# Other start addresses for the operands of the down projection in a one-core decoder layer

## The chip, the cores and the metric

The kernel runs on one core of a Trainium2 chip. The metric is the device time of one execution in microseconds; where several runs are given, the median counts. Before the change, three runs took 328.39, 328.74 and 328.99 us.

## The reference

One hybrid decoder layer on 256 tokens of width 1024, all in float32. The part that matters here is its last third, the gated feed-forward network with a causal convolution of three taps:

```python
h2 = rmsnorm(x, norm_ffn_g)
up = causal_depthwise_conv(h2 @ w_up, conv_w, conv_b)
gate, val = jnp.split(up, 2, axis=-1)
return x + (jax.nn.silu(gate) * val) @ w_down
```

`w_up` is 1024 x 5632 and `w_down` 2816 x 1024. Ahead of it stand the projections of queries, keys, values, pooling input and gates, an attention of 8 heads, a causal pooling mixer, two branch projections and the output projection.

## The kernel before

**Every product is made of three.** Each float32 operand is split into a rounded high part and the rest, a low part, both in the one-pass format `float32r`. ACT writes the high part (`high`, L91), DVE the low part (`low`, L95 and L97), and TensorE adds three matmuls into one accumulator: high x high, and the two mixed products. So weights arrive by DMA in a `raw` tile and are held as a `hi_` and a `lo_` tile. From the pooling input on, the weights are the stationary operand (128 x 128) and the activations, transposed, the moving operand (128 partitions x 256 tokens). For queries, keys and values it is the other way round: there the weights move, 512 columns or, in the first two of eight steps of the queries, 256 columns at a time.

**Weights come in chunks of 1 MB** in one fixed order. In the feed-forward part the order alternates up chunks (22, one per block of 128 gate and 128 value features) and down chunks (11, each for two blocks of 128 of the 2816 features). Four buffers each hold raw, high and low parts and rotate. The function `ahead` lets ACT and DVE split chunks ahead of their use; `chunk` hands the next one to the matmuls.

**The feed-forward loop** runs i from 0 to 21. Each turn makes two up tiles, gate and value, of 24 matmuls each (3 x 8 slices of the depth), whose moving operands are `hhi` and `hlo`. DVE, ACT and POOL apply the norm's factor, the taps, the silu and the product of gate and value. `value_done` then has ACT write the high part of the result, `ah`, and `finish`, one turn later, has POOL write the low part, `al`: 256 columns of 4 bytes, 1,024 bytes in each partition. `LAG` is 3: in turn i, the matmuls of `down(i - 3)` follow the up tiles. One such block has 24 matmuls: for each of eight output slices, `hi` x `ah`, `hi` x `al` and `lo` x `ah` (L866 to L868). Block i uses down chunk i // 2, its first half for even i. Blocks 0 to 17 are followed by up tiles; 18 to 21 come at the end, the last two interleaved slice by slice. `ah` and `al` have `LAG + 2` = 5 buffers each, which rotate.

**The order of the work** on each engine is the order in which the program is written; an engine's instructions are chained so. Nothing is reordered by a planner.

**Places in memory.** Tiles lie at fixed bytes in each partition, given by the allocator in the order of the pools. The kernel shifts some operands inside their tiles by whole words of 4 bytes: `MOVING` (48 words) for the weights of queries, keys and values, `FAR` (96 words) for all other low parts. The starts before, in bytes modulo 128, as they stand in the built program:

| operand | start modulo 128 |
|---|---|
| `xhi`, `xlo`, `hhi`, `hlo`, `mh`, `ml`, `ah`, `al` and the other activations | 96 |
| high and low parts of the weights of queries, keys, values | 96 |
| high and low parts of all other weights | 32 |
| `ones_r` (two matmuls into `ps_n`, for the second norm) | 0 |

Steps inside a weight tile from one 128-column slice to the next are 512 bytes, so all slices of a tile start alike modulo 128.

Of the kernel before, what the change touches and what calls it, by code (L numbers as in the profile page):

```python
# [8 lines left out]
F32R = mybir.dt.float32r  # L9
# [4 lines left out]
P = 128  # L14
S = 256
# [31 lines left out]
LAG = 3  # L47
# [17 lines left out]
FAR = 96  # L65
MOVING = 48
XCUTS = (1, 2, 3, 4, 5, 6, 8)


@with_exitstack  # L70
def hybrid_layer_kernel(ctx: ExitStack, tc: tile.TileContext, xq_d, xtok_d, par_d, wkv_d, wpg_d,
# [12 lines left out]
    tmp = mixer.enter_context(tc.tile_pool(name="tmp", bufs=2))  # L84
# [5 lines left out]
    def high(hi, src, scale=1.0):  # L90
        nc.scalar.activation(hi, src, AF.Copy, scale=scale)  # L91
# [16 lines left out]
    order = [("q", None)] * 2 + [("k", wkv_d[c]) for c in range(2)]  # L108
# [28 lines left out]
    def raw(c, sl):  # L137

        if order[c][0] != "q":
            return raws[c][:, sl]  # L140
        at = sl.start % 512
        return xq[:, 4 * c + sl.start // 512, S + at:S + at + sl.stop - sl.start]
# [7 lines left out]
    for c in range(len(order) - 1):  # L150
        if order[c][0] == "dn" and order[c + 1][0] == "up":
            i = next(n for n, p in enumerate(pieces) if p[0] == c)
# [7 lines left out]
    def oldest():  # L160

        return next((c for c in range(len(order)) if c not in spent), len(order))

    def next_high():
        if at[0] < len(pieces):
            c, sl, first, _ = pieces[at[0]]
            if c - oldest() >= WBUFS:
                return
            at[0] += 1
            if first:  # L170
                moving = order[c][0] in "qkv"
                place = MOVING if moving else 0
                his[c] = whi_p.tile([P, CH + P], F32R, tag="whi", name=f"hi_{order[c][0]}{c}")[:, place:]
                place = MOVING if moving else FAR
                los[c] = wlo_p.tile([P, CH + P], F32R, tag="wlo", name=f"lo_{order[c][0]}{c}")[:, place:]
            high(his[c][:, sl], raw(c, sl))

# [21 lines left out]
    def ahead(upto=0):  # L199

        next_high()
        next_low()
        if at[1] - sum(p[0] < used[0] for p in pieces) < upto:
            next_high()
            next_low()
# [23 lines left out]
    cut = 0  # L229
    for k in XCUTS:  # L230
        end = KD + k * (S + AW)
# [32 lines left out]
    for k in range(KD):  # L264
        if k < HALVED:
            nc.vector.tensor_scalar(xhi[:, k, :], xT[:, k, :], gmix[:, k:k + 1], None, op0=ALU.mult)
        else:
            high(xhi[:, k, :], xT[:, k, :], gmix[:, k:k + 1])
        low(xlo[:, k, :], xhi[:, k, :], xT[:, k, :], gmix[:, k:k + 1])
        for _ in range(2 if k < HALVED else 1):  # L270
            next_high()
        for _ in range(2 if k < HALVED else 1):
            next_low(eager=True)
# [403 lines left out]
    for n in range(2 * KD):  # L677
# [13 lines left out]
        b, c = n // 2, n % 2  # L691
# [9 lines left out]
        f = 2 * GATES[b] + c  # L701
# [41 lines left out]
    tmp = ctx.enter_context(tc.tile_pool(name="ffn", bufs=2))  # L743
# [71 lines left out]
    acch, accl = {}, {}  # L815
# [12 lines left out]
    def taps(u, f, c):  # L828
        cw = [par[:, C_CW + j * 2 * KF + f:C_CW + j * 2 * KF + f + 1] for j in range(3)]
        nc.vector.scalar_tensor_tensor(c[:, 1:S], u[:, 0:S - 1], cw[1], c[:, 1:S], ALU.mult, ALU.add)  # L830
        nc.vector.scalar_tensor_tensor(c[:, 2:S], u[:, 0:S - 2], cw[0], c[:, 2:S], ALU.mult, ALU.add)  # L831
# [14 lines left out]
    def value_done(i, g, uc):  # L846
        taps(uc[0], KF + i, uc[1])
        nc.gpsimd.tensor_tensor(uc[1], g[1], uc[1], ALU.mult)  # L848
        acch[i] = tmp.tile([P, S], F32R, tag="ah", bufs=LAG + 2, name=f"ah{i}")
        accl[i] = tmp.tile([P, S], F32R, tag="al", bufs=LAG + 2, name=f"al{i}")  # L850
        high(acch[i], uc[1])
        return uc[1]

# [44 lines left out]
    ahead()  # L898
    gate_done(0, ug)
    done = value_done(0, ug, uv)  # L900
    for i in range(1, KF):
        if i > 1:
            w = chunk("up")
            ps = [up_tile(w, 0, i)]
        ug = normed(ps[0], i, f"g{i}")
        ahead()
        finish(i - 1, done)
        ps.append(up_tile(w, 1, i))
        uv = normed(ps[1], KF + i, f"v{i}")
        gate_done(i, ug)  # L910
        ahead()
        if i >= LAG:
            if i == LAG:
                pairs.close()
                down_p = ctx.enter_context(tc.tile_pool(name="down", bufs=1, space=bass.MemoryType.PSUM))
                acc += [down_p.tile([P, 512], F32, name=f"ps_d{n}") for n in range(4)]
            down(i - LAG, range(KD))
            ahead(FFN_AHEAD)
        done = value_done(i, ug, uv)
# [6 lines left out]
    for m in (0, 2, 4, 6, 1, 3, 5, 7):  # L926
        for i in (KF - 2, KF - 1):
            down(i, (m,))
        o = acc[m // 2][:, (m % 2) * S:(m % 2 + 1) * S]
# [76 lines left out]
```

## Time and profile before

| | us |
|---|---|
| median of 3 runs | 328.74 (328.39 to 328.99) |
| the profiled execution | 328.95 |
| its span, first to last instruction | 327.2 |
| PE busy (matmul) | 322.8 |
| DVE busy | 259.4 |
| ACT busy | 201.6 |
| POOL busy | 71.8 |

Each row of a view by groups gives the line, the engine, the operation, out<-in by the program's tile names, the shape, the count, the busy time, the mean duration of one in ns, and the idle time of the engine just before. Rows in order of time begin with the start and the duration in us; several equal instructions in succession are one row with their count, which gives the start of the first. Matmuls overlap by design, so the pace of PE is the distance from one start to the next. PE is the matrix engine's matmuls, PEld its weight loads.

### The profile page before, as it was taken

To read this page: it belongs to the slowest core of one execution; us is meant where nothing else is said; L and a number is where in the kernel's file an instruction comes from. 1 tells how busy PE (TensorE), PEld (TensorE's weight loads), DVE (VectorE), ACT (ScalarE), POOL (GpSimd) and SP (SyncE) were. 2 spreads that over 40 slices of the span, in tenths; PEclk is the share of its full clock that TensorE was granted. 3 is DMA by queue.
4 is the path that set the end of the run, shared out by engine and by line. 5 is a ranking of instruction groups with operands and counts; after the bars stand their busy time and mean duration, and the time that the engine had idled before them with its cause. 6 is when DMAs were issued, how large, how long until landed. Compare 5 with 4: busy or idle time off the path is not lost.

```text
span 327.2 us, 6768 instructions
## 1 busy us (share of the span) xinstructions
PE 322.8 (99%) x2708; PEld 316.1 (97%) x2708; DVE 259.4 (79%) x447; ACT 201.6 (62%) x329; POOL 71.8 (22%) x89
## 2 busy tenths in 40 slices
PE   8999999999999999999999999999999999999995
PEld 8888899999999999999999999999999999999995
DVE  4939989989988966879997978686868686868834
ACT  5767519665995657669675647474747474746520
POOL 1007690000000151230421221212121212121330
PEclk9999999999999999999999999999999999999999
DMA  7999799837799833735527456464645454643003
GB/s 258 422 412 240 218 385 284 299 138 268 270 255 312 372 128 131 241 146 179 207 97 290 179 207 221 165 214 175 214 172 217 170 213 173 221 165 130 0 2 128
DMA packets 16542, 69.72 MB, mean 213 GB/s; under 512 B 2176, under 2 KB 7040, under 8 KB 9856
## 3 DMA queue, kind: packets, MB, share of 16 engines
q1 hardware_dynamic: 16096, 69.17, 59.5%
q8 instruction: 21, 0.34, 0.4%
q10 hardware_dynamic: 416, 0.13, 0.2%
q14 instruction: 9, 0.07, 0.1%
HBM read 65.61 MB, written 3.69 MB: 212 GB/s over the span
## 4 chain that ended last, share of the span: by engine, by line
PE 99%; DVE 0%; issue 0%
PE ps_up L104 12%; PE ps_up L103 12%; PE ps_up L105 12%; PE ps_d L867 6%; PE ps_d L866 6%; PE ps_d L868 6%; PE ps_g L103 5%; PE ps_g L104 4%; PE ps_g L105 4%; PE ps_q L333 4%; PE ps_k L333 3%; PE ps_v L333 3%; PE ps_out L104 2%; PE ps_out L105 2%; PE ps_out L103 2%; PE ps_warm L248 1%
## 5 line engine op out<-in xcount | busy, mean ns | idle before, releaser
L105 PE MATMUL ps_up<-hhi,lo_up 128*128 128x256 f32 x352 | 97.3, 276 | 0.0
L104 PE MATMUL ps_up<-hlo,hi_up 128*128 128x256 f32 x352 | 97.3, 276 | 0.0
L103 PE MATMUL ps_up<-hhi,hi_up 128*128 128x256 f32 x352 | 97.3, 276 | 0.0
L104 PEld LDWEIGHTS ps_up<-hlo,hi_up 128*128 128x128 f32 x352 | 66.1, 188 | 0.0
L103 PEld LDWEIGHTS ps_up<-hhi,hi_up 128*128 128x128 f32 x352 | 66.1, 188 | 0.0
L105 PEld LDWEIGHTS ps_up<-hhi,lo_up 128*128 128x128 f32 x352 | 66.1, 188 | 0.0
L95 DVE TENSOR_TENSOR lo_up<-raw_up,hi_up 128x1024 fp32r<-128x1024 f32 x44 | 54.7, 1262 | 7.3 <-ACT hi_up L91 7.3
L867 PE MATMUL ps_d<-al,hi_dn 128*128 128x256 f32 x176 | 48.6, 276 | 0.0
L868 PE MATMUL ps_d<-ah,lo_dn 128*128 128x256 f32 x176 | 48.6, 276 | 0.0
L866 PE MATMUL ps_d<-ah,hi_dn 128*128 128x256 f32 x176 | 48.6, 276 | 0.0
L91 ACT ACTIVATE hi_up<-raw_up 128x1024 fp32r<-128x1024 f32 x44 | 44.1, 1046 | 0.0
L848 POOL TENSOR_TENSOR c_v<-c_g,c_v 128x256 f32<-128x256 f32 x22 | 16.2, 737 | 121.4 <-DVE c_v L831 121.4
L91 ACT ACTIVATE ah<-c_v 128x256 fp32r<-128x256 f32 x22 | 9.2, 418 | 45.6 <-POOL c_v L848 45.6
L103 PE MATMUL ps_g<-xhi,hi_g 128*128 128x256 f32 x128 | 35.6, 278 | 0.0
L105 PE MATMUL ps_g<-xhi,lo_g 128*128 128x256 f32 x128 | 35.4, 277 | 0.0
L104 PE MATMUL ps_g<-xlo,hi_g 128*128 128x256 f32 x128 | 35.4, 277 | 0.0
L866 PEld LDWEIGHTS ps_d<-ah,hi_dn 128*128 128x128 f32 x176 | 33.1, 188 | 0.0
L867 PEld LDWEIGHTS ps_d<-al,hi_dn 128*128 128x128 f32 x176 | 33.1, 188 | 0.0
L868 PEld LDWEIGHTS ps_d<-ah,lo_dn 128*128 128x128 f32 x176 | 33.0, 188 | 0.0
L95 DVE TENSOR_TENSOR lo_dn<-raw_dn,hi_dn 128x1024 fp32r<-128x1024 f32 x22 | 27.8, 1263 | 0.4 <-ACT hi_dn L91 0.4
L836 DVE TENSOR_TENSOR u_v<-ps_up,R 128x256 f32<-128x256 f32 x22 | 9.3, 422 | 20.9 <-PE ps_up L105 20.8
L873 POOL TENSOR_TENSOR al<-c_v,ah 128x256 fp32r<-128x256 f32 x22 | 22.0, 1002 | 11.6 <-ACT ah L91 11.6
(196 smaller groups left out, 781.5 us busy)
## 6 DMA issues: line engine op xcount, KB each, us to landing
raw_up<-in_wup SPq DMA_DIRECT2D x22, 1024.0 KB, 4.8
raw_g<-in_wpg SPq DMA_DIRECT2D x8, 1024.0 KB, 7.3
raw_dn<-in_wdn SPq DMA_DIRECT2D x8, 1024.0 KB, 4.9
raw_o<-in_wout SPq DMA_DIRECT2D x4, 1024.0 KB, 10.1
raw_dn<-in_wdn SPq DMA_DIRECT2D x6, 512.0 KB, 4.8
raw_v<-in_wkv SPq DMA_DIRECT2D x2, 1024.0 KB, 15.3
raw_p<-in_wpg SPq DMA_DIRECT2D x2, 1024.0 KB, 12.8
raw_bp<-in_wbp SPq DMA_DIRECT2D x2, 1024.0 KB, 5.5
```

What stands on the lines that cost most here:

```text
L91: nc.scalar.activation(hi, src, AF.Copy, scale=scale)
L95: nc.vector.tensor_tensor(lo, src, hi.bitcast(F32), ALU.subtract)
L103: nc.tensor.matmul(out, sh, mh, start=start, stop=False, **kw)
L104: nc.tensor.matmul(out, sh, ml, start=False, stop=False, **kw)
L105: nc.tensor.matmul(out, sl, mh, start=False, stop=stop, **kw)
L333: nc.tensor.matmul(pt[t][:, c:c + wide], sx[:, k, t * P:(t + 1) * P], wx[:, sl], start=k == 0 and c == 0 and sx is xhi and wx is hi, stop= ...
L836: nc.vector.tensor_tensor(u, ps[:, 0:S], R2, ALU.mult)
L848: nc.gpsimd.tensor_tensor(uc[1], g[1], uc[1], ALU.mult)
L866: nc.tensor.matmul(o, hi[:, sl], acch[i], start=first, stop=False, skip_group_check=True)
L867: nc.tensor.matmul(o, hi[:, sl], accl[i], start=False, stop=False, skip_group_check=True)
L868: nc.tensor.matmul(o, lo[:, sl], acch[i], start=False, stop=i == KF - 1, skip_group_check=True)
L873: nc.gpsimd.tensor_tensor(accl[i], act_i, acch[i].bitcast(F32), ALU.subtract)
```

## The change

The activations `ah` and `al` no longer share one tag of five buffers each. They get ten tags with one buffer, 288 instead of 256 words wide, and start 8, 8, 24, 24 or 0 words into it, by i modulo 5. Of the weights of the down projection, every other chunk (the second, the fourth, and so on; five of eleven) has its high part 8 words (32 bytes) and its low part 24 words (96 bytes) further on. The starts of these operands, in bytes modulo 128, are now:

| operand | start modulo 128 |
|---|---|
| `ah`, `al` for i modulo 5 = 0, 1 | 0 |
| `ah`, `al` for i modulo 5 = 2, 3 | 64 |
| `ah`, `al` for i modulo 5 = 4 | 96 |
| `hi_dn`, `lo_dn`, even chunk | 32 |
| `hi_dn`, odd chunk | 64 |
| `lo_dn`, odd chunk | 0 |

The order of the instructions, their number, their waits and all other places stay as they were. Line numbers after the change are two to four higher.

```diff
+AH_AT = (8, 8, 24, 24, 0)
+AL_AT = (8, 8, 24, 24, 0)
...
                 moving = order[c][0] in "qkv"
-                place = MOVING if moving else 0
+                further = 8 * (order[c][0] == "dn" and sum(o[0] == "dn" for o in order[:c]) % 2)
+                place = MOVING if moving else further
                 his[c] = whi_p.tile([P, CH + P], F32R, tag="whi", name=f"hi_{order[c][0]}{c}")[:, place:]
-                place = MOVING if moving else FAR
+                place = MOVING if moving else FAR + 3 * further
                 los[c] = wlo_p.tile([P, CH + P], F32R, tag="wlo", name=f"lo_{order[c][0]}{c}")[:, place:]
...
     def value_done(i, g, uc):
         taps(uc[0], KF + i, uc[1])
         nc.gpsimd.tensor_tensor(uc[1], g[1], uc[1], ALU.mult)
-        acch[i] = tmp.tile([P, S], F32R, tag="ah", bufs=LAG + 2, name=f"ah{i}")
-        accl[i] = tmp.tile([P, S], F32R, tag="al", bufs=LAG + 2, name=f"al{i}")
+        b = i % (LAG + 2)
+        acch[i] = tmp.tile([P, S + 32], F32R, tag=f"ah{b}", bufs=1, name=f"ah{i}")[:, AH_AT[b]:AH_AT[b] + S]
+        accl[i] = tmp.tile([P, S + 32], F32R, tag=f"al{b}", bufs=1, name=f"al{i}")[:, AL_AT[b]:AL_AT[b] + S]
         high(acch[i], uc[1])
         return uc[1]
```

## The prediction

> **What bounds the kernel now.** I read the page first: the span of 327.2 us, the share of each engine, and the chain that ended last. The profiled execution took 328.95 us, so 1.75 us lie around its span. The median of the three timed runs is 328.74 us, 0.21 below the profiled one, and I carry every difference over to that median.
>
> ```profile
> PE 322.8 (99%) x2708; PEld 316.1 (97%) x2708; DVE 259.4 (79%) x447; ACT 201.6 (62%) x329; POOL 71.8 (22%) x89
> PE 99%; DVE 0%; issue 0%
> L867 PE MATMUL ps_d<-al,hi_dn 128*128 128x256 f32 x176 | 48.6, 276 | 0.0
> L868 PE MATMUL ps_d<-ah,lo_dn 128*128 128x256 f32 x176 | 48.6, 276 | 0.0
> L866 PE MATMUL ps_d<-ah,hi_dn 128*128 128x256 f32 x176 | 48.6, 276 | 0.0
> ```
>
> The matmuls are the whole chain. The last three rows are the down projection, the only matmuls whose operands the change moves: 3 x 176 = 528 of them. Their 276 ns overlap, since matmuls are pipelined, so what a matmul costs must be read from start to start. The list of waits has one entry for PE, at the very beginning:
>
> ```profile
> PE ps_warm L248 <- DVE ones L216: 1.1, 1, 1.1
> ```
>
> So PE waits for no engine and no transfer afterwards. What remains to set the time is the pace at which it takes matmuls. The order of time shows one block of the down projection, from its first matmul to the first of the up projection behind it:
>
> ```profile
> 255.72 0.28 PE L866 MATMUL ps_d<-ah,hi_dn 128*128 128x256 f32 x1
> ...
> 258.44 0.28 PE L103 MATMUL ps_up<-hhi,hi_up 128*128 128x256 f32 x1
> ```
>
> That is 2.72 us for 24 matmuls, 113.3 ns each. The chain of waits gives the same pace for 512 columns, twice 113.3:
>
> ```profile
> 16.90 10.88 PE ps_k L333 x48
> ```
>
> 10.88 us / 48 = 226.7 ns. So the pace is steady, and 0.44 ns a column without anything fixed per matmul.
>
> **Where the trace shows another pace.** Two stretches differ from 113.3 ns at 256 columns, with PE waiting for nothing. The first is in the q projection:
>
> ```profile
> 6.63 0.64 PE L333 MATMUL ps_q<-lo_q,xhi 128*128 128x256 f32 x4
> 7.11 0.28 PE L333 MATMUL ps_q<-hi_q,xhi 128*128 128x256 f32 x1
> ...
> 8.08 0.64 PE L333 MATMUL ps_q<-lo_q,xhi 128*128 128x256 f32 x4
> 8.55 0.41 PE L333 MATMUL ps_q<-hi_q,xhi 128*128 128x512 f32 x1
> ```
>
> Sixteen matmuls lie between 6.63 and 8.55: 1.92 us, 120.0 ns each, 6.7 ns more. The second is where two matmuls on `ones_r` are put between matmuls of the up projection:
>
> ```profile
> 148.53 0.29 PE L105 MATMUL ps_up<-hhi,lo_up 128*128 128x256 f32 x1
> 148.66 0.28 PE L887 MATMUL ps_n<-sh,ones_r 128*128 128x256 f32 x1
> 148.78 0.28 PE L887 MATMUL ps_n<-sl,ones_r 128*128 128x256 f32 x1
> 148.89 0.28 PE L103 MATMUL ps_up<-hhi,hi_up 128*128 128x256 f32 x1
> ...
> 150.43 0.28 PE L104 MATMUL ps_up<-hlo,hi_up 128*128 128x256 f32 x1
> 150.55 0.28 PE L105 MATMUL ps_up<-hhi,lo_up 128*128 128x256 f32 x1
> ```
>
> The operands of these two had long been written:
>
> ```profile
> 147.23 0.42 ACT L91 ACTIVATE sh<-ss 128x256 fp32r<-128x256 f32 x1 [0.58 <-DVE ss L791]
> 147.68 0.43 DVE L95 TENSOR_TENSOR sl<-ss,sh 128x256 fp32r<-128x256 f32 x1 [0.48 <-ACT sh L91]
> ```
>
> Both end by 148.11, and the first `ps_n` starts at 148.66. Still the steps around it are 130, 120 and 110 ns, and from 148.89 to 150.43 thirteen matmuls take 1.54 us (118.5 ns each) before 113 returns. The q projection has weights and moving operand at the same place modulo 128 bytes (both at 96); `ones_r` lies at 0 with the moving operand at 96. Everywhere the pace is 113.3 at 256 columns, moving operands start at 96 and weights at 32: **64 bytes apart modulo 128**. Two places depart from that distance, and both are slower. This is a correlation over two stretches of one trace, and the q stretch is also the start of the program, with other engines writing; but it is what the trace has.
>
> **The change, part by part.** It adds, removes and moves no instruction, transfer or wait. The two programs issue the same work in the same order; only start addresses differ, on 528 matmuls and their weight loads, 32 ACT writes, 22 POOL writes and 10 DVE writes. *ACT, DVE, POOL:* at 62, 79 and 22% they have room, and PE waits for none of them, so a slightly other write time is hidden behind PE; I cost it at 0. If it were not hidden, 64 writes at a tenth of the 418 ns of an `ah` write would be 2.7 us, but no PE wait shows from which they could surface.
>
> ```profile
> L91 ACT ACTIVATE ah<-c_v 128x256 fp32r<-128x256 f32 x22 | 9.2, 418 | 45.6 <-POOL c_v L848 45.6
> ```
>
> *Tile rotation:* five buffers under one tag become five tags with one buffer, the buffer of index i still being that of i - 5. Cost 0.
>
> *The reads of PE.* Modulo 128, the five places of `ah` and of `al` are now 0, 0, 64, 64, 96; even chunks of weights stay at 32 (both `hi` and `lo`), odd chunks have `hi` at 64 and `lo` at 0. Index i uses place i mod 5 and chunk i // 2. Going through i = 0 to 21, each 24 matmuls, 16 with `hi` and 8 with `lo`:
> - even chunk, place at 0 or 64 (i = 0, 1, 5, 8, 12, 13, 16, 17, 20, 21): none of 240 is 64 apart;
> - even chunk, place at 96 (i = 4, 9): all 48 stay 64 apart;
> - odd chunk, place at 64 (i = 2, 3, 7, 18): `hi` is 0 apart, 64 matmuls off;
> - odd chunk, place at 0 (i = 6, 10, 11, 15): `lo` is 0 apart, 32 off;
> - odd chunk, place at 96 (i = 14, 19): all 48 off.
>
> So 240 + 64 + 32 + 48 = 384 matmuls leave the distance of 64. [...] Above: the `ps_n` step that grew to about 123 to 130 ns, some 10 more at least. I take the q row, +6.7 ns, as it is the longest steady stretch: 384 x 6.7 = 2.6 us.
>
> *The way back to the pace.* Each block is followed by 48 up matmuls whose own addresses have not changed. After `ps_n` the return cost 1.54 - 13 x 0.1133 = 0.07 us. The cheapest return in the trace is behind the v projection, also with weights and moving operand at one place:
>
> ```profile
> 38.50 0.28 PE L103 MATMUL ps_u<-xhi,hi_p 128*128 128x256 f32 x1
> ...
> 38.97 0.28 PE L104 MATMUL ps_u<-xlo,hi_p 128*128 128x256 f32 x1
> ```
>
> four steps in 0.47, 0.02 over. Blocks i = 0 to 17 without 4 and 9 are followed by up matmuls: 16 x 0.045 (the middle) = 0.7 us, between 0.3 and 1.1. **Sum:** 2.6 + 0.7 = +3.3 us, 328.95 + 3.3 = 332.25 for a profiled execution and 328.74 + 3.3 = **332.0 us** for the median. With all 20 altered blocks at +10 ns (480 x 10 = 4.8, and 1.1) it is +5.9, 334.6; with the pace kept inside the blocks and only entries and returns paid (32 x 0.02) +0.6.
>
> **The rivals.** *Faster: the moving operand on a multiple of 64 is read without the loss.* [...] Eighteen of 22 blocks get such an operand: 432 x 6.6 = 2.9 us less; with half of that and the returns of 0.7 paid, 0.7 less: 325.9 to 328.0, some 327.0. [...] It decides as soon as an aligned `ps_d` block takes under 2.70 us.
>
> [...]
>
> *No change: the place does not matter.* PE takes contiguous columns wherever they begin, q was slow because of the start of the program, and `ps_n` because its weights came from another tile. For it: 113.3 holds for `hi` and `lo` alike, which differ by 128 bytes. Against it: `ps_n`, far from the start and waiting for nothing. It gives 328.7.
>
> [...]
>
> *Nothing is shifted:* the altered addresses stand in the built program on all 528 matmuls, so I give that nothing.
>
> **Chances.** Slower by the distance 0.61, its own range 329.4 to 334.6; faster 0.25; no change 0.14. A measurement of this kernel tells about 0.2% (0.66 us) from nothing, and the three cases lie beyond, beyond and within it. The range from 326.8 to 334.2 leaves out the better half of the gain (0.12) and the top of the loss (0.07).
>
> **What would show it.** In the profile after, PE still at 99% with no new wait, the other engines as before, ps_up at 113.3 well behind each block, and blocks i = 4 and 9 at 2.72 us while 0, 1, 5 and 8 take 2.72 + 24 x 0.0067 = 2.88 us. Blocks under 2.70 prove the faster rival; all blocks at 2.72 prove that places are free. A wait of PE for `ah` or `lo_dn` would show that a write was not hidden. Blocks that differ, but by another rule than the distance of 64, would leave the sign and break the count of 384.

## The result and the profile after

| | before | after |
|---|---|---|
| median us | 329.46 (18 runs) | 332.66 (18 runs) |
| ratio | | 1.0117, 95% interval 1.0096 to 1.0139 |
| profiled execution, span | 327.2 | 331.5 |

The ratio is taken over undisturbed runs alone, the medians over all. The change makes the kernel 1.2% slower; on the 328.74 us of the first three runs the ratio is +3.8 us (3.2 to 4.6). The page after: the engines, one group of the up projection and the three of the down projection (columns as before):

```profile
PE 325.8 (98%) x2708; PEld 318.8 (96%) x2708; DVE 259.5 (78%) x447; ACT 201.6 (61%) x329; POOL 72.8 (22%) x89
L106 PE MATMUL ps_up<-hlo,hi_up 128*128 128x256 f32 x352 | 97.4, 277 | 0.0
L870 PE MATMUL ps_d<-ah,hi_dn 128*128 128x256 f32 x176 | 49.7, 282 | 0.0
L872 PE MATMUL ps_d<-ah,lo_dn 128*128 128x256 f32 x176 | 49.6, 282 | 0.0
L871 PE MATMUL ps_d<-al,hi_dn 128*128 128x256 f32 x176 | 49.3, 280 | 0.0
```

ACT and DVE have their old busy time to 0.1 us, POOL 1.0 more. Each down matmul lasts 4 to 6 ns longer than the 276 of before, and PE waits for none of their operands. The list of waits of PE after the change:

```profile
PE ps_warm L251 <- DVE ones L219: 1.1, 1, 1.1
PE ps_ba L106 <- DVE heads L97: 0.9, 1, 0.9
PE ps_q L336 <- ACT hi_q L93: 0.5, 1, 0.5
```

The second and third stand far ahead of the changed part. The wait at `ps_ba` stands in three of the fourteen traces of this case, and in one of them, of a kernel whose down projection is as fast as before, it is 1.9 us. I therefore count the change in the trace by itself, from start to start: the sum, over all matmuls of a group, of the distance to the next start less 113.33 ns. For the 528 down matmuls it was 0.00 us before and is 2.81 after; for the 1056 up matmuls 0.08 before and 0.77 after. Together **+3.5 us**. The span's other 0.8 are in the main the `ps_ba` wait and what hangs on it (1.25 us in all there), less 0.5 at the first matmuls of q.

Two blocks of the profile after, in order of time, each with its first matmul and the first of the up projection behind it:

```profile
166.83 0.28 PE L870 MATMUL ps_d<-ah,hi_dn 128*128 128x256 f32 x1
...
169.66 0.28 PE L105 MATMUL ps_up<-hhi,hi_up 128*128 128x256 f32 x1
...
200.09 0.28 PE L870 MATMUL ps_d<-ah,hi_dn 128*128 128x256 f32 x1
...
202.97 0.29 PE L105 MATMUL ps_up<-hhi,hi_up 128*128 128x256 f32 x1
```

Block 0 takes 2.83 us, 118.2 ns a matmul. Block 4, whose operands the prediction had left at 113.3, takes 2.88 us, 120.0. Read so, the mean pace of all blocks, beside the one that the prediction's count gives them, is:

| blocks | starts modulo 256: `hi`, `lo`, `ah`, `al` | predicted ns | measured ns |
|---|---|---|---|
| 0, 1, 5, 16 | 32, 160, 0, 128 | 120.0 | 118.2 |
| 8, 12, 13, 17 | 32, 160, 64, 192 | 120.0 | 118.7 |
| 4, 9 | 32, 160, 224, 96 | 113.3 | 120.0 |
| 2, 3, 7, 18 | 64, 0, 64, 192 | 117.8 | 117.8 |
| 6, 10, 11, 15 | 64, 0, 0, 128 | 115.5 | 119.1 |
| 14, 19 | 64, 0, 224, 96 | 120.0 | 119.5, 119.1 |

(20 and 21, interleaved, are at 118.1 to 118.5.) The pace goes with the places: blocks with the same four starts agree to 0.1 ns on the mean, and their steps repeat matmul by matmul, whatever other engines do meanwhile. What ran just before counts too: block 19, which follows another down block, differs from block 14.

### The profile page after: what moved, and what is told of

Read it like the earlier page. It is cut to its first block, busy times and chain, and to the rows that moved or that the text cites. A ratio compares the mean times of both kernels' runs of the same rounds, so it can differ in the third digit from the quotient of the medians.

```text
span 331.5 us, 6768 instructions
## 1 busy us (share of the span) xinstructions
PE 325.8 (98%) x2708; PEld 318.8 (96%) x2708; DVE 259.5 (78%) x447; ACT 201.6 (61%) x329; POOL 72.8 (22%) x89
## 4 chain that ended last, share of the span: by engine, by line
PE 93%; DMA 3%; DVE 2%; ACT 0%; issue 0%; ACTq 0%
PE ps_up L107 12%; PE ps_up L105 12%; PE ps_up L106 12%; PE ps_d L872 6%; PE ps_d L870 6%; PE ps_d L871 6%; PE ps_g L105 5%; PE ps_g L106 4%; PE ps_g L107 4%; PE ps_q L336 3%; PE ps_k L336 3%; PE ps_v L336 3%; PE ps_out L107 2%; PE ps_out L106 2%; PE ps_out L105 2%; DMA raw_ba<-in_wba 2%
## 5 line engine op out<-in xcount | busy, mean ns | idle before, releaser
L870 PE MATMUL ps_d<-ah,hi_dn 128*128 128x256 f32 x176 | 49.7, 282 | 0.0
L872 PE MATMUL ps_d<-ah,lo_dn 128*128 128x256 f32 x176 | 49.6, 282 | 0.0
L871 PE MATMUL ps_d<-al,hi_dn 128*128 128x256 f32 x176 | 49.3, 280 | 0.0
L877 POOL TENSOR_TENSOR al<-c_v,ah 128x256 fp32r<-128x256 f32 x22 | 23.5, 1067 | 11.6 <-ACT ah L93 11.6
```

Source lines behind the costliest of these rows:

```text
L870: nc.tensor.matmul(o, hi[:, sl], acch[i], start=first, stop=False, skip_group_check=True)
L871: nc.tensor.matmul(o, hi[:, sl], accl[i], start=False, stop=False, skip_group_check=True)
L872: nc.tensor.matmul(o, lo[:, sl], acch[i], start=False, stop=i == KF - 1, skip_group_check=True)
L877: nc.gpsimd.tensor_tensor(accl[i], act_i, acch[i].bitcast(F32), ALU.subtract)
```

## The experiments

Theory 1 is the prediction's: 64 bytes modulo 128 between a matmul's own weights and moving operand. Theory 2, from blocks 4 and 9, is that moving operands which follow each other must start alike modulo 256: the new tiles of 288 words, 1,152 bytes, put `al` 4.5 x 256 bytes behind `ah`.

**The two halves of the change apart.** First the weights alone (`ah`, `al` as before):

```diff
-        b = i % (LAG + 2)
-        acch[i] = tmp.tile([P, S + 32], F32R, tag=f"ah{b}", bufs=1, name=f"ah{i}")[:, AH_AT[b]:AH_AT[b] + S]
-        accl[i] = tmp.tile([P, S + 32], F32R, tag=f"al{b}", bufs=1, name=f"al{i}")[:, AL_AT[b]:AL_AT[b] + S]
+        acch[i] = tmp.tile([P, S], F32R, tag="ah", bufs=LAG + 2, name=f"ah{i}")
+        accl[i] = tmp.tile([P, S], F32R, tag="al", bufs=LAG + 2, name=f"al{i}")
```

> Only the odd down chunks are shifted (high part 32, low part 96 bytes further); ah and al lie as before. Theory 1 (what counts is that a matmul's moving operand and weights start 64 bytes apart modulo 128): the 10 blocks with an odd chunk are all off that distance, 120 ns a matmul there (160 ns more a block), 113.3 in the 12 even ones; with the returns about +2.0 us. Theory 2 (the moving operands that follow each other must start alike modulo 256; weights are free): all blocks 113.3, +0.0 us.

Ratio 1.0067 (1.0012 to 1.0122); in the trace +1.4 us. Up to block 19, the even-chunk blocks are at 113.3 ns and the odd ones at 117.8. Blocks 0 and 2, in order of time:

```profile
165.40 0.28 PE L869 MATMUL ps_d<-ah,hi_dn 128*128 128x256 f32 x1
...
168.12 0.28 PE L105 MATMUL ps_up<-hhi,hi_up 128*128 128x256 f32 x1
...
181.72 0.28 PE L869 MATMUL ps_d<-ah,hi_dn 128*128 128x256 f32 x1
...
184.55 0.28 PE L105 MATMUL ps_up<-hhi,hi_up 128*128 128x256 f32 x1
```

2.72 against 2.83 us. Weights are not free: theory 2 alone falls. Then the activations alone:

```diff
-                further = 8 * (order[c][0] == "dn" and sum(o[0] == "dn" for o in order[:c]) % 2)
-                place = MOVING if moving else further
+                place = MOVING if moving else 0
...
-                place = MOVING if moving else FAR + 3 * further
+                place = MOVING if moving else FAR
```

> Only ah and al lie at the ten new places; the weights lie as before. Theory 1: blocks with i mod 5 = 4 at 113.3 ns (i = 4, 9, 14, 19), the other 18 at 120, about +3.5 us. Theory 2: as the new tiles put al 128 bytes from ah modulo 256, all 22 blocks are slow, 117 to 120 ns, about +3.5 us too; blocks 4, 9, 14, 19 tell the two apart.

Ratio 1.0121 (1.0102 to 1.0139), in the trace +3.9 us, more than the whole change. All 22 blocks are slow, those with i modulo 5 = 4 most, at 120.0 (block 19, behind another down block, at 120.2). Block 4 in order of time:

```profile
199.36 0.28 PE L869 MATMUL ps_d<-ah,hi_dn 128*128 128x256 f32 x1
...
202.24 0.29 PE L105 MATMUL ps_up<-hhi,hi_up 128*128 128x256 f32 x1
```

It takes 2.88 us though all its operands are 64 bytes apart modulo 128: theory 1 alone falls.

**Ten tags without an offset, and `al` put back.** Weights as before in both:

```diff
-AH_AT = (8, 8, 24, 24, 0)
-AL_AT = (8, 8, 24, 24, 0)
+AH_AT = (0, 0, 0, 0, 0)
+AL_AT = (0, 0, 0, 0, 0)
```

and, in the second run,

```diff
-AL_AT = (0, 0, 0, 0, 0)
+AL_AT = (32, 32, 32, 32, 32)
```

> Ten tags and tiles of 288 words, but all offsets 0 and the weights as before: ah stays at 224 modulo 256, al moves from 224 to 96, all still 64 apart from the weights modulo 128. Theory 1: nothing changes, 113.3 in all blocks, +0.0 us. Theory 2: al no longer starts like ah modulo 256, all blocks near 120 ns as in blocks 4 and 9 of the change, +3.5 us with 40 ns for each return.

> As the run with ten tags and no offset, but al begins 32 words into its tile, so that ah and al both start at 224 modulo 256 again (they differ by 256 modulo 512). Both theories: 113.3 in all blocks, +0.0 us. If the period is 512 bytes and not 256, it stays near 120 ns, +3.5 us. If the tags or the tiles' width cost something by themselves, it is slower too.

Without an offset, 1.0131 (1.0114 to 1.0148), +4.3 us in the trace; all blocks between two up tiles at 120.0 ns. With `al` back at 224 modulo 256, 1.0023 (0.9992 to 1.0054), and 113.3 ns in all 22 blocks, 0.0 us in the trace. Block 0 of each, without an offset and with `al` back:

```profile
166.28 0.28 PE L869 MATMUL ps_d<-ah,hi_dn 128*128 128x256 f32 x1
...
169.16 0.29 PE L105 MATMUL ps_up<-hhi,hi_up 128*128 128x256 f32 x1
```

```profile
170.25 0.28 PE L869 MATMUL ps_d<-ah,hi_dn 128*128 128x256 f32 x1
...
172.97 0.28 PE L105 MATMUL ps_up<-hhi,hi_up 128*128 128x256 f32 x1
```

2.88 and 2.72 us. One constant moves it by 160 ns a block. The tags and widths cost the matmuls nothing, and a period of 256 bytes fits: here `ah` and `al` differ by 256 modulo 512 and are at 113.3 ns, in the run before they differ by 128 and are at 120.0. It is the run that had the 1.9 us at `ps_ba`.

**Two surveys.** Since a block's pace repeats, one run can hold 22 different placements; each survey is one profiled execution, read in its trace and not by its time. Tables give the start of each operand modulo 256, in tiles of 320 words (5 x 256 bytes):

```diff
+def words(start, base):
+    return (start - base) % 256 // 4
...
+                down_n = sum(o[0] == "dn" for o in order[:c])
+                is_down = order[c][0] == "dn"
+                place = MOVING if moving else words(HI_START[down_n], 32) if is_down else 0
...
+                place = MOVING if moving else words(LO_START[down_n], 32) if is_down else FAR
...
+        ha, la = words(AH_START[i], 224), words(AL_START[i], 224)
+        acch[i] = tmp.tile([P, S + 64], F32R, tag=f"ah{b}", bufs=1, name=f"ah{i}")[:, ha:ha + S]
+        accl[i] = tmp.tile([P, S + 64], F32R, tag=f"al{b}", bufs=1, name=f"al{i}")[:, la:la + S]
```

> A survey: the starts of the down operands, modulo 256, are set block by block, so one run gives 22 samples of 24 matmuls. Even blocks 2 to 14 shift all four operands together by 32, 64, ... 224 (weights high 32 + s and low 160 + s, ah = al = 224 + s); odd blocks 3 to 15 have the same weights with ah = al = 224. Theory 3 (only distances between moving operand and weights modulo 256 count): all even blocks 2 to 14 at 113.3 ns, and the odd ones slow except where the distance repeats. Theory 4 (places count by themselves, 224 for what moves, 32 and 160 for weights): even blocks 2 to 14 slow, 117 to 120. Blocks 16 and 18 have weights at 32 and 32, and at 160 and 32, with the usual 224: if the pair of weights load and the matmul that streams meanwhile counts, 16 is slow and 18 is open; blocks 0, 17 and 19 have ah = al = 96.

> A second survey. Blocks 0 to 13 have high weights at 32 and low weights at 192, 224, 0, 32, 64, 96, 128 modulo 256, two blocks each: the even block with ah = al = 224, the odd one with al 64 bytes beyond the low weights. Theory 3a (what counts is where the next weights are loaded from while a matmul streams: high weights 64 beyond ah, low weights 192 beyond al): all odd blocks at 113.3 ns, the even ones slow, 117 to 120. Theory 3b (each matmul with its own weights): odd blocks slow as well, as al is no longer 64 below the high weights. Blocks 14 and 15 move al alone (to 32, 160), 16 and 17 ah alone (to 160, 32): slow under both.

"Settled" means 113.3 ns from some matmul to the end of the block.

| first survey: blocks | `hi`, `lo`, `ah` = `al` | ns over the block |
|---|---|---|
| 2, 4, 6, 8, 10, 12, 14 | 32 + s, 160 + s, 224 + s | 115.4, 114.0, 113.5, 114.0, 115.7, 114.3, 114.0; settled after 9, 4, 0, 3, 10, 3, 3 matmuls |
| 9 and 18; 16 | 160, 32, 224; 32, 32, 224 | 113.3, settled at once |
| 3, 5, 7, 11, 13, 15 | other distances, 224 | 117.7 to 121.1, never settled |
| 19 | 160, 32, 96 | 114.0, settled after 3 |
| 0; 17 | 32, 160, 96; 32, 32, 96 | 118.8; 117.8, never settled |
| 1 | 32, 160, `ah` 96, `al` 224 | 117.7, never settled |

In the second survey only block 6 of blocks 0 to 19 settles (low weights at 32, `ah` = `al` = 224). All with `al` off `ah` are slow, 115.5 to 120.0, among them block 7, in which every operand is 64 from the weights modulo 128 and `al` is at 96. Theory 3a, with `al` following the low weights, falls with the odd blocks 1 to 13.

So in blocks 2 to 14 the distances count and not the places by themselves, and the conditions of theories 1 and 2 are **both needed**: every block that settles meets both within itself. Block 2 of the first survey has its moving operands on a multiple of 64 (0) and its weights 64 and 192 beyond. Its tenth matmul, and the first of the up projection 15 matmuls later:

```profile
183.21 0.28 PE L878 MATMUL ps_d<-ah,hi_dn 128*128 128x256 f32 x1
...
184.91 0.28 PE L111 MATMUL ps_up<-hhi,hi_up 128*128 128x256 f32 x1
```

1.70 us / 15 = 113.3 ns. Matmuls whose moving operand starts on a multiple of 64 settle at the same pace, not a faster one. And the distances do not suffice: blocks 0 and 17, with moving operands 128 bytes from the up projection's 224, keep them and do not settle within 24 matmuls, while blocks 8 and 19, equally far from 224, do.

**The old distances at multiples of 64, in all blocks.**

```diff
+HI_START = (64, 64, 64, 64, 64, 64, 64, 64, 64, 64, 64)
+LO_START = (192, 192, 192, 192, 192, 192, 192, 192, 192, 192, 192)
+AH_START = (0, 0, 0, 0, 0, 0, 0, 0, 0, 0, 0, 0, 0, 0, 0, 0, 0, 0, 0, 0, 0, 0)
+AL_START = (0, 0, 0, 0, 0, 0, 0, 0, 0, 0, 0, 0, 0, 0, 0, 0, 0, 0, 0, 0, 0, 0)
...
```

> All down blocks have ah = al = 0 modulo 256, multiples of 64 bytes, with weights at 64 and 192: the old distances, shifted by 32. If distances alone set the pace: each block pays its entry only and settles at 113.3 (as block 2 of the first survey, 115.4 ns over the block, 49 ns), each return 17 ns: 22 x 0.049 + 18 x 0.017 = +1.4 us. If multiples of 64 were read faster, the settled pace would be under 113.3; if they are slow by themselves, the blocks stay at 118 and it is +3.5 us.

1.0051 (1.0016 to 1.0086), in the trace +1.25 us: 0.93 in the blocks and 0.32 in the returns. Every block that follows an up tile takes 115.4 ns and is settled from its tenth matmul; the returns cost 17 or 18 ns. What is left of the loss is entry and return. With moving operands on multiples of 64, as in most blocks of the change, but without the mismatch, the trace loses a third as much (1.25 against 3.5 us).

**The rule on another product.** The down projection as before, the low weights of the up projection 32 bytes further on:

```diff
-                place = MOVING if moving else FAR
+                place = MOVING if moving else FAR + 8 * (order[c][0] == "up")
```

> The down projection lies as before; the low weights of the up projection start 32 bytes further on (192 modulo 256 instead of 160), so that 352 of its 1056 matmuls leave the distance. If the rule is of PE's reads and not of the down projection: all 22 up pairs take the pace of block 0 of the second survey, which had these four places (117.1 ns: 1056 x 3.8 = +4.0 us), and each down block pays for the way back, 15 to 70 ns; +4.2 to +5.2 us in all. If only the shifted third pays: 352 x 6.7 = +2.4 us at most.

1.0147 (1.0091 to 1.0202), +4.8 us; in the trace +4.6. One turn, from the first up matmul to the next:

```profile
270.14 0.28 PE L103 MATMUL ps_up<-hhi,hi_up 128*128 128x256 f32 x1
...
275.76 0.28 PE L866 MATMUL ps_d<-ah,hi_dn 128*128 128x256 f32 x1
...
278.52 0.28 PE L103 MATMUL ps_up<-hhi,hi_up 128*128 128x256 f32 x1
```

48 up matmuls in 5.62 us, 117.1 ns; 24 untouched down matmuls in 2.76, 115.0. The survey's 117.1 carried over, and the two thirds of the up matmuls with unchanged places slowed down like the shifted third (117.2 and 117.4 ns against 116.6 on the mean): the matmuls beside a disturbed one slow down with it.

**The two slow stretches of before.** `ones_r` alone, 32 bytes further on, and, in another run, `ones_r` together with the moving weights of q, k and v (`MOVING = 32` in place of 48):

```diff
-    ones_r = const.tile([P, P], F32R, name="ones_r")
+    ones_r = const.tile([P, P + 64], F32R, name="ones_r")[:, 8:8 + P]
```

> The kernel before with one edit: ones_r starts 32 bytes further on, at 160 instead of 128 modulo 256, so that the two matmuls on it have the distance that the others have. Distances as cause: the steps into and out of ps_n stay at 113 ns and the slow stretch behind them is gone, 0.08 us less in the trace, no difference that the time can tell. It is the only place of the kernel before, beside the sixteen matmuls of q and those behind the attention's matmuls, that is not at 113.3.

> The kernel before, with the two places repaired that departed from the distance of 64 modulo 128: the moving weights of q, k and v start at 160 instead of 224 (64 below their weights' 224), and ones_r at 160 instead of 128. The down projection is as before. If the distance is a cause and not a mere company of the slow stretches: the sixteen 256-column matmuls of q at 113.3 ns instead of 120 (0.1 us less), the steps into and out of ps_n at 113 and no slow stretch behind them (0.08 us less); in all -0.2 us, less than a time can tell, so the trace decides. If q was slow because of the start of the program, it stays at 120.

With `ones_r` alone, 0.9997 (0.9981 to 1.0013). The same stretch in order of time:

```profile
148.78 0.28 PE L105 MATMUL ps_up<-hhi,lo_up 128*128 128x256 f32 x1
148.89 0.28 PE L887 MATMUL ps_n<-sh,ones_r 128*128 128x256 f32 x1
149.01 0.28 PE L887 MATMUL ps_n<-sl,ones_r 128*128 128x256 f32 x1
149.12 0.28 PE L103 MATMUL ps_up<-hhi,hi_up 128*128 128x256 f32 x1
...
150.59 0.28 PE L104 MATMUL ps_up<-hlo,hi_up 128*128 128x256 f32 x1
```

Thirteen steps from 149.12 take 1.47 us, 113.3 each, where before they took 1.54. So the places of `ones_r` made that stretch. No run beat the kernel before by more than can be measured: apart from such stretches its 256-column matmuls of 128 rows are at the settled pace, and no block of any run was below that.

In q the expectation held for half. The other run's matmuls of q in order of time:

```profile
5.80 0.62 PE L333 MATMUL ps_q<-hi_q,xlo 128*128 128x256 f32 x4
6.26 0.62 PE L333 MATMUL ps_q<-lo_q,xhi 128*128 128x256 f32 x4
6.71 0.64 PE L333 MATMUL ps_q<-hi_q,xhi 128*128 128x256 f32 x4
7.19 0.64 PE L333 MATMUL ps_q<-hi_q,xlo 128*128 128x256 f32 x4
7.66 0.64 PE L333 MATMUL ps_q<-lo_q,xhi 128*128 128x256 f32 x4
8.13 0.63 PE L333 MATMUL ps_q<-hi_q,xhi 128*128 128x512 f32 x2
```

Eight matmuls in 0.91 us, 114 ns; then the next twelve in 1.42, 118 ns, with the same distances. The first of the twelve steps is 124 ns long; what made it was not shown. The pace was lost there and did not come back.

Nor was the 120 ns of q a matter of the start of the program. In the other thirteen traces, whose q weights lie as before, its last twelve matmuls of 256 columns take 119.5 to 120.1 ns on the mean, whether none or eight of its first ones had taken 213 ns. The run with tiles of 320 words, below, has left its beginning by 5.84:

```profile
5.84 0.64 PE L335 MATMUL ps_q<-hi_q,xlo 128*128 128x256 f32 x4
...
8.24 0.63 PE L335 MATMUL ps_q<-hi_q,xhi 128*128 128x512 f32 x2
```

Twenty matmuls in 2.40 us are 120.0 ns each.

**Steps below 32 bytes.** The tables of the surveys again:

> A third survey, in steps below 32 bytes. Blocks 0, 2, 4, 6: weights 4, 8, 16 bytes further on or 16 back, with ah = al = 224; blocks 1, 3, 5, 7: all four shifted together by as much. Blocks 8 to 11: al alone shifted by 4, 8, 16, -16; 12 and 13: ah and al together by 8 and -8; 16: as before; 14, 15, 17: weights at 160 and 160 with 224 and 96, and the usual weights with 96. If the exact distance counts: 1, 3, 5, 7 and 16 at 113.3, the other shifted ones slow. If whole lines of 32 bytes count: 0, 2, 4, 8, 9 and 13 stay in a line of the first place or leave it together by the line alone, so 0, 2 and 4 are at 113.3 and 6 is slow.

Neither theory held. Blocks 14 (weights at 160 and 160) and 16, both with 224, are at 113.3. All others of blocks 0 to 17 are slow, 116.7 to 121.9, even those with all four operands shifted together by 4, 8 or 16 bytes: block 1 is at 121.1. So within 24 matmuls a shift by a part of 32 bytes does not settle even at the old distances; whether it would in a longer run was not tried. Block 15 (160, 160, 96) keeps the distances and does not settle, at 118.0; block 17 repeats block 0 of the first survey, matmul by matmul, at the same 118.8.

**Both conditions at the change's own offsets.** Tiles of 320 words and the change's ten offsets, weights as before:

```diff
-        acch[i] = tmp.tile([P, S + 32], F32R, tag=f"ah{b}", bufs=1, name=f"ah{i}")[:, AH_AT[b]:AH_AT[b] + S]
-        accl[i] = tmp.tile([P, S + 32], F32R, tag=f"al{b}", bufs=1, name=f"al{i}")[:, AL_AT[b]:AL_AT[b] + S]
+        acch[i] = tmp.tile([P, S + 64], F32R, tag=f"ah{b}", bufs=1, name=f"ah{i}")[:, AH_AT[b]:AH_AT[b] + S]
+        accl[i] = tmp.tile([P, S + 64], F32R, tag=f"al{b}", bufs=1, name=f"al{i}")[:, AL_AT[b]:AL_AT[b] + S]
```

> The change's ten offsets for ah and al with the weights as before, in tiles of 320 words instead of 288, so that al starts like ah modulo 256 in every place. What is left is the distance to the weights, by the two surveys: places 0 and 1 (ah = al = 0: high weights 32, low weights 160 beyond) like block 15 of the first survey, 118.1 ns with 69 ns for each return; places 2 and 3 (224 and 96 beyond) like block 11, 119.0 with 35; place 4 (64 and 192 beyond) settled at 113.3 from its first matmul. Sum: 10 x 24 x 4.8 + 8 x 24 x 5.7 = 2.2 us, returns 8 x 0.069 + 7 x 0.035 = 0.8, +3.0 us. Blocks 4, 9, 14, 19 above 113.3, or the others at another pace than in the survey, would say that distances and equal moving starts do not describe it.

1.0096 (1.0061 to 1.0131), in the trace +2.4 us. Block 4 and block 2 in order of time:

```profile
198.83 0.28 PE L869 MATMUL ps_d<-ah,hi_dn 128*128 128x256 f32 x1
...
201.55 0.28 PE L105 MATMUL ps_up<-hhi,hi_up 128*128 128x256 f32 x1
```

```profile
182.24 0.28 PE L869 MATMUL ps_d<-ah,hi_dn 128*128 128x256 f32 x1
...
185.09 0.28 PE L105 MATMUL ps_up<-hhi,hi_up 128*128 128x256 f32 x1
```

By i modulo 5, the blocks of 4 are at 113.3 (2.72 us), those of 0 and 1 at 118.4 against 118.1 expected, those of 2 and 3 at 118.9 against 119.0. The distances give the pace within 0.3 ns at other absolute places. They do not give the returns: 13 and 1 ns here, 69 and 35 in the survey, which is the part that +3.0 us had too large. What sets the cost of a return was not shown.

## Why the prediction was right, and where it was wrong

- **Sign and size:** +3.3 us was forecast, 332.0; measured +3.8 (3.2 to 4.6), 332.66, and +3.5 in the trace. PE set the time, no new wait came from the changed writes, and the cause was the pace of the matmuls: 118.7 ns on the mean of the down projection, against 113.3.
- **The step that failed is the count of 384** by "64 bytes modulo 128" between a matmul's own operands. It named a needed condition and took it for the only one. The other, equal starts modulo 256 of the moving operands that follow each other, was broken in all 22 blocks by the tile width of 288 words, which the prediction did not look at. Blocks 4 and 9, its own test, were at 120.0 instead of 113.3. It also let a matmul keep its pace beside disturbed ones; they slow down together, as the shifted up weights show (117.2 and 117.4 ns beside the shifted 116.6).
- **The price of 6.7 ns** was too high for most: 2.81 us / 528 = 5.3 ns on the mean. 384 x 6.7 = 2.6 and 528 x 5.3 = 2.8 are close because a count too small met a price too large. That the sum came out is luck in this part.
- **The returns,** 0.7 by 16 x 0.045, measured 0.69 over 18 returns. Singly they run from -1 to 73 ns, so the middle of two rows was a fair mean and no more. The two stretches that the prediction named were also not all: in the trace before, behind the first score product of the attention, twelve matmuls of `ps_g` from 67.36 us on take 118.5 ns each, a return like that behind `ps_n`.
- **The faster rival** fell on the run with all four operands moved together: aligned moving operands settled at 113.3, never below. No run shows the 6.6 ns a matmul that its sum counts on: no block of any run was below 113.3 on the mean.
- **No change** fell too: all operands of the first two surveys start on multiples of 32 bytes, and their blocks range from 113.3 to 121.1 ns.
- **q as evidence:** `ps_n` was rightly read, which the moved `ones_r` confirms. For q the places count too: with weights and moving operand at one place it ends at 120 ns in thirteen traces, so its start was not the cause. But the distance of 64 gave 113.3 for eight matmuls only.

## What to carry to other kernels

When PE is busy to the end and waits for nothing, read its matmuls from start to start: here 113.3 against 116 to 122 ns at 256 columns of `float32r`, 2 to 8%, hung on start addresses alone. Keep tile widths at multiples of the address period seen (256 bytes here: with the old weights, block 4 was at 120.0 ns in tiles of 1,152 bytes and at 113.3 in tiles of 1,280), so that adding or splitting buffers does not move one operand against another, and compare the starts of two builds before looking for a lost wait. A placement that settles is worth most if it is the same for all products, since in the run with all four operands moved together the blocks, though they settled at 113.3, paid 0.93 us for their entries and 0.32 for the returns.

## What the runs showed of the hardware

In these runs the pace of a stream of weight loads and matmuls had a settled state, 113.33 ns at 256 columns, and repeating slower patterns of 116 to 122 ns on the mean. Places, and what ran just before, went with the pattern matmul by matmul: blocks of the change with the same four starts agree to 0.1 ns on the mean, and block 19, behind another down block, is at 119.1 where block 14 is at 119.5. A stream that had left the settled state found back within 13 matmuls in the up projection of the change; in the q of the run with `MOVING = 32`, at 118 ns, it did not within twelve. One slower state is as even as the settled one: blocks 1 and 17 of the first survey, block 2 of the second, blocks 7 and 15 of the third and that q run at 117 to 119 ns in every step, 117.7 to 117.9 on the mean of a block once they are in it, with different distances.

At 512 columns the better of the two distances tried is the other one. The chain of waits of the run with `MOVING = 32`:

```profile
16.69 11.20 PE ps_k L333 x48
```

11.20 / 48 = 233.3 ns, where the same matmuls took 226.7 with weights and moving operand at one place. In order of time, a weight load of that run ends ahead of its matmul:

```profile
20.04 0.42 PEld L333 LDWEIGHTS ps_k<-lo_k,xhi 128*128 128x128 f32 x2
20.27 0.63 PE L333 MATMUL ps_k<-lo_k,xhi 128*128 128x512 f32 x2
```

The load begins at 20.04 and lasts 0.19 us (the row holds two), so it ends at 20.23, 0.04 us before the matmul starts at 20.27, as in the kernel before. That a late weight load costs the 6.7 ns at 512 columns is thus not shown, nor what else does. Open too are why no block settled below 113.33 and why a moving operand 128 bytes from its neighbours' place settles with one pair of weights and not with another.
